# One order of work for another: the two written sequences of a transformer block

## The chip, the cores and the metric

The kernel runs on one core of a Trainium2 chip. The metric is the device time of one execution in microseconds (us). Five engines matter: TensorE (PE in the profile; its weight loads are PEld), VectorE (DVE), ScalarE (ACT), GpSimd (POOL) and SyncE (SP), which here only issues DMAs. SP and POOL each have a queue of DMAs that go out in order. Each engine runs its own instructions in order and waits on semaphores for the others.

## The reference

One block on 512 tokens of width 1024, in fp32: a norm, one wide projection, a gated linear attention (GLA, 4 heads) and a latent attention (MLA, 8 heads) side by side, their gated sum through `w_out`, then a squared-ReLU MLP of width 4096 and a last norm.

```python
n = rmsnorm(h, g_mix)
proj = n @ w_in
(gq, gk, gv, gr, z_gf, z_gb, cq, ckv, kr, z_ma, z_mb) = jnp.split(proj, SPLIT_IDX, axis=-1)
y_gla = gla_branch(gq, gk, gv, gr, z_gf, z_gb, ...)
y_mla = mla_branch(cq, ckv, kr, positions, g_q, w_uq, g_kv, w_ukv)
merged = jax.nn.sigmoid(z_ma) * y_gla + jax.nn.sigmoid(z_mb) * y_mla
h = h + merged @ w_out
m = rmsnorm(h, g_mlp)
h = h + jnp.square(jax.nn.relu(m @ w_ff1)) @ w_ff2
return rmsnorm(h, g_final)
```

In `mla_branch` each head has 64 features without and 32 with rotary position; `cq` and `ckv` are normed and then multiplied up to queries, keys and values; each head takes a softmax over all 512 tokens.

## The kernel before

Every fp32 matrix is held as a rounded upper part and a rest (names in h and l), and each product is three matmuls (`mm3`: high by high, high by low, low by high). The large products (projections, `w_out`, the MLP) use a scheme with seven half-size products instead of eight, so their operands are sums of blocks (names such as bo10 to bo71 for the right operands of `w_out`, gao, gbo, gco, gdo, yo, zo for the left).

What sets the order: nothing is scheduled. While `nc.hold()` is on, each call on an engine is recorded under a letter and the name of its first tile (`P` TensorE, `A` ScalarE, `D` VectorE, `G` GpSimd, `S` SyncE's DMAs; `D:h0` is VectorE's next recorded call that writes h0). `nc.emit(SEQUENCE)` then issues the recorded calls as the string names them, `*3` meaning three in a row, and `in_program_order` keeps each engine to that order. So only the place of an entry among the entries of the same letter matters, and each queue stands still while its first entry waits. SEQUENCE covers the stretch from the last GLA head to the first products of the MLP; LAST_ROWS covers the last rows of the MLP and the final norm.

What is in the stretch, with the names that matter:

- `up_units(pr)` makes queries, keys and values for the heads 2pr and 2pr+1. Its weights come through a stage buffer (`stage`, three buffers in all, also used by `streamed` for the weights bo.. of `w_out`), are split (wq..h/l, wk..h/l), and give uq, uk and uv in PSUM. The rotary part of q is copied by DMA from ro (`rotary_rows`), the other head's half of q and of the keys (kbuf) by DMA too. For the last pair, pr = 3, the weights of q are wq3f; the keys lie in four tiles kbuf0 to kbuf3, of which heads 4 to 7 reuse those of heads 0 to 3.
- `att_scores` computes s (head, block of 128 queries), VectorE's row maximum top and ScalarE's exponential e with its sum tot; `att_normalise` takes the reciprocal and scales e, one block on ScalarE and one on VectorE; `att_flip` transposes e into tp and splits it into pT (ScalarE high, VectorE low); `att_values` gives av, `merge` gates it (tb, VectorE) and adds the GLA part on GpSimd into mx and my; `merged_sums` forms yo and zo from these.
- `wo_product` adds the products with bo.. into the accumulators wox, wow and woz (a bank each for row block 0 and 1); `add_rows` adds a full bank into h on VectorE (`D:h0`), after which the bank may be used anew.
- Then the MLP's norm: ScalarE squares the rows of h with their sum (ms), VectorE combines (hp), GpSimd raises hp to the power −1/2, VectorE and ScalarE scale the rows (ms again), and TensorE flips them into the banks mb. The flipped rows are split into mh and ml for f0x, the MLP's first product.
- `load_onto` adds a block of weights in DRAM onto a tile in SBUF with an accumulating DMA from GpSimd's queue (`G:w2_20`); plain loads go through SyncE's queue.

Of the kernel before, what the change touches and what calls it, by code (L numbers as in the profile page):

```python
# [97 lines left out]
def tile_block(ctx: ExitStack, tc: tile.TileContext, t, out: bass.AP):  # L98
# [1784 lines left out]
    for x in range(2):  # L1883
        f0.lo(2, x)
        m_lo(2, x)
    SEQUENCE = """
# [5 lines left out]
        A:tb4 P:ro1*9 S:wk1f D:ckvhl1 A:zb7h D:sc1 D:gla3s D:rob0 D:rob1 D:sc0 D:zb7l P:zb6*24 A:wk1h S:wq2f
        A:kbuf0 G:wk1l A:ckvhl0 D:kbuf0 A:wk1h D:roa0 S:kbuf2 G:wk1l P:uq0*9 D:roa0 S:w2_11 A:q010 G:wk0l A:ro0
        G:wk0l P:gla3o0*12 D:ro0 G:wk0l D:ckvhl0 S:q001 P:gla3o1*12 S:w2_10 D:roa1 P:gla3o1*6 S:q000 D:roa1
        P:gla3o0*6 S:kbuf1 A:ro1 S:q010 A:gla3sq D:ro1 A:wk1h P:uk0*6 S:q000 G:wk1l A:kbuf0 S:q001 G:wk0l A:wk1h
        S:q010 A:tb5 S:q111 A:q000 A:gla3sq S:wq2f D:q001 A:kbuf1 S:q011 D:q011 A:gla3sq*2 S:wq1f D:zb6 A:yg4
        G:gla3ss*2 S:wq1f D:kbuf0 G:gla3ss S:wq1f G:wk1l D:grc P:zb7*24 S:wq2f D:zb7 S:q011 P:s00*3 D:grb S:q111
        D:kbuf1 S:w2_20 D:grc P:uv01*12 D:top00 S:q210 A:v01 P:s03*3 D:grb S:bo11f A:wq1h A:e00 P:s01*3 S:q110
        G:wq1l D:top01 A:wq2h S:bo11f D:v01 G:wq2l S:bo10f P:uk1*6 D:top03 A:kbuf2 P:y16*4 A:yg6 S:wk2f P:y17*4
        A:e03 P:s11*3 S:w2_00 D:top11 A:e01 S:kbuf3 P:s02*3 S:q211 A:e11 D:tot00 P:s10*3 S:w2_30 D:top10 A:e00  # L1900
        S:q110 D:top02 A:e10 S:w2_01 D:kbuf2 A:e02 P:uq1*9 A:q100 D:tot02 P:s13*3 A:yg7 S:q110 P:s12*3 A:bo11h
        D:q101 S:kbuf3 D:e01 S:q111 D:top13 S:bo10f P:uv10*12 D:tot10 D:bo11l P:tp000*4 S:q210 A:pT000 P:tp001*3
        A:e02 D:top12 S:wk3f A:e13 D:pT010 S:q100 P:uv00*12 P:tp001 P:uq2 A:v00 S:q100 A:e12 D:v00 S:q101 A:e10
        D:tot12 D:e03 S:kbuf2 A:wk2h P:uq2*8 D:e13 A:wk2h G:wk2l S:q101 A:pT001 G:wk2l S:w2_00 A:wk2h A:e12 S:w2_01
        G:wk2l P:uv11*12 P:tp010*4 S:q211 A:pT000 P:s31*3 A:v10 D:top31 P:tp011*4 A:tb7 D:pT010 A:e31 D:e11 P:uk2*6
        D:pT011 A:pT001 P:tp101*4 A:q200 D:pT011 P:tp100*4 A:wk3h S:q210 A:pT101 D:v10 P:s21*3 A:pT100 D:q201
        P:s20*3 A:wk2h P:av0 D:top20 A:kbuf0 S:q211 G:wk2l D:top21 A:wk3h S:w2_20 A:v11 S:w2_10 D:pT111 A:e20
        S:bo21f D:kbuf0 P:av0*11 A:e21 S:q200 D:pT110 P:tp110*4 S:kbuf1 D:tot20 A:pT100 D:e21 P:s23*3 A:bo10h
        S:q201 D:top23 P:s22*3 S:q201 D:pT110 A:e23 P:tp111*4 D:top22 A:pT101 D:tb0 A:e22 P:uv21*12 D:pT111 G:mx0
        A:e20 P:s30*3 D:tot22 A:e22 G:my0 D:top30 P:s32*3 D:bo10l G:w2_20 A:e30 P:tp200*4 G:wk3l A:pT200 S:wq3f  # L1910
        D:pT210 S:kbuf0 D:e23 S:q200 D:top32 P:av1*12 S:wq3f D:tb1 A:e32 P:tp201*4 S:wq3f P:s33*3 G:my0 A:wk3h
        A:pT201 S:q311 D:top33 P:tp210*4 G:mx0 A:v21 S:q311 D:v11 P:s53*3 A:pT200 S:bo21f D:pT211 A:e33 S:q310
        D:v21 A:wk3h P:uv20*12 S:h2 D:pT210 A:wq3h P:tp211*4 S:q300 D:top53 G:wq3l P:s41*3 S:q310 P:av2 D:tot30
        D:e31 A:e53 S:q301 P:s40*3 G:wk3l A:e30 D:tot32 D:top41 S:w2_30 A:pT201 G:wk3l D:top40 S:q301 P:av2*5 A:tb6
        G:w2_00 P:uq3 S:w2_31 P:tp301*4 G:wk3l A:pT301 S:bo20f A:e41 S:w2_21 D:pT311 A:e40 S:w2_21 P:uq3*8 S:q300
        P:tp300*4 D:tot40 D:pT211 A:pT300 S:w2_11 P:s51*3 A:q300 D:top51 S:w2_31 P:s43*3 D:e33 S:bo20f A:e51
        P:s42*3 D:top43 S:w221f A:v20 D:pT310 A:e32 P:av2*5 D:top42 D:v20 P:s52*3 A:e42 D:q301 P:tp311*4 A:pT301
        D:e41 A:e43 D:top52 P:uv30*12 A:gao0 D:pT311 A:e52 P:s50*3 G:gao0 P:av2 A:e40 D:tb2 P:tp310*4 A:pT300
        D:tot52 D:tot42 G:yo0 D:e43 A:q310 P:uk3*6 G:mx1 D:pT310 A:kbuf3 P:tp400*4 D:q311 A:kbuf2 G:w2_21 P:tp401*4
        A:pT400 D:top50 G:yo0 A:pT401 D:kbuf2 A:e42 D:kbuf3 G:my1 A:e50 D:pT411 G:zo0 P:av3*12 A:v30 D:tb3 P:s70*3  # L1920
        D:pT410 G:my1 P:tp410*4 A:pT400 D:tot50 D:top70 P:s60*3 G:w2_20 A:e50 D:pT410 P:tp411*4 G:zo1 A:pT401 D:v30
        A:e70 D:top60 G:mx1 P:uv31*12 A:e52 D:pT411 G:yo1 A:e60 P:s61*3 P:av4 D:top61 G:yo1 A:gdo0 P:s63*3 A:bo50h
        D:e51 D:top63 P:s62*3 A:e61 D:top62 P:wox0*3 A:e63 D:tot60 P:tp501*4 D:e53 A:e62 D:bo50l P:wox1*3 A:pT501
        P:tp511*4 D:tot62 A:gao1 D:e61 S:w2_00 P:s71*3 D:pT511 A:ghyo0 G:gao1 S:h0 A:pT501 D:top71 P:av4*4 S:h1
        A:bo21h D:gdo0 P:s72*3 S:h3 G:zo1 D:pT511 A:e71 D:top72 G:glyo0 A:e60 P:av4*7 D:tb4 P:tp500*4 A:pT500
        P:tp510*4 D:tot70 D:e63 G:my2 A:pT500 D:pT510 P:s73*3 P:wox0 A:e72 D:pT510 G:mx2 P:wox0*2 A:e62 D:bo21l
        P:tp601*4 G:w2_11 A:v31 P:tp600*4 P:av5 A:pT601 G:w2_21 P:av5*2 D:top73 A:pT600 G:zo0 P:tp610*4 A:e70
        D:pT610 A:pT600 D:pT611 A:ghyo1 G:zo2 D:e71 A:e73 P:av5*9 D:tb5 P:tp611*4 A:pT601 D:tot72 D:pT610 P:wox1*3
        G:my2 A:gdo0 P:tp700*4 D:pT611 A:ghzo1 G:glyo1 P:tp701*4 P:av6 D:v31 A:pT701 D:e73 A:pT700 G:mx2 A:bo20h
        D:pT710 G:yo2 D:pT711 A:e72 P:av6*11 G:w2_01 D:bo20l A:f010h P:av7*5 G:yo2 A:gao2 D:tb6 P:av7*7 D:gao2  # L1930
        G:w2_10 P:wow0*3 G:mx3 P:tp710*4 A:pT700 P:wow0*3 A:ghyo2 G:zo2 D:pT710 P:tp711*4 A:pT701 G:my3 P:wox1*3
        A:gao3 P:wox0*3 D:gao3 D:gdo0 P:woz1*3 D:tb7 D:pT711 G:mx3 P:wox0*3 D:f010l P:wox1*3 A:bo60h G:w2_00 A:gao3
        D:bo60l P:av7*12 P:wow1*3 D:gao3 P:wow0*3 D:zo3 D:tb7 P:woz0*3 D:glyo2 G:my3 P:wow1*3 A:bo61h P:wow0*3
        G:w2_20 D:yo3*2 P:woz1*3 G:glzo1 D:h0 P:woz0*3 D:h1 A:bo51h D:zo3 P:wow1*3 P:wox0*3 A:ghbo3 D:bo51l A:ghco3
        P:wox0*3 D:glbo3 P:wow1*3 S:w2_01 A:bo31h D:h0 P:woz0*3 D:h1 P:woz0*3 A:ms0 D:bo31l A:gdo2 P:wox1*3 G:hp0
        A:ms1 P:wox1*3 D:bo61l A:ghzo0 S:w2_31 P:woz1*3 A:bo71h G:glzo0 D:h2 P:woz1*3 A:bo30h D:h3 P:wox0*3 G:hp1
        G:w2_21 P:wox1*3 A:ghzo2 D:bo30l A:f011h P:wox0*3 D:glco3 P:wox1*3 S:w2_30 A:bo70h D:glzo2 S:w220f D:h0
        D:bo70l P:woz0*12 D:bo71l D:h1 S:w2_11 A:bo40h D:h0 S:w2_10 P:woz1*12 A:ms0 D:h1 A:gdo2 D:hp0 D:bo40l A:ms1
        G:hp0 P:wox1*6 A:f050h D:ms0 A:ms0 D:hp1 D:f011l G:hp1 P:wox0*12 G:w2_01 A:ms1 P:mb02 P:mb01 D:h2 P:mb03
        A:bo41h D:ms1 D:gdo2 P:wox1*6 D:gdo2 P:mb03 P:mb02 P:mb00 P:mb01 D:bo41l P:mb00 P:mb02 P:mb01 P:mb00*2  # L1940
        P:mb02 P:mb03 A:mr20 P:mb03 P:mb01 D:h3 A:mr10 A:mr21 D:f050l A:mr11 A:ms2 A:mr10 G:w2_00 A:mr11 A:mr21
# [128 lines left out]
```

## Time and profile before

| | before |
|---|---|
| runs (us) | 737.14, 738.35, 738.58; median 738.35 |
| the profiled execution (us) | 737.48 |
| its span, first to last instruction (us) | 735.8 |
| granted clock of TensorE | 0.998 |
| mean DMA rate | 149 GB/s |

The span is what the rows of the profile lie in, from 0 to 735.8; the 1.7 us around it have no rows. The stretch that SEQUENCE orders lies between about 253 and 422 us. Rows give the start, the duration, the engine, the source line (held calls all have L76, the line in `emit`), the operation, the names out<-in without buffer numbers, and in brackets the idle time just before with what ended it. TensorE's rows overlap, since matmuls are pipelined: the step from one start to the next is the cost, not the duration.

### The profile page before, as it was taken

Reading aid. Unit: us, or ns where it says so; the run is one execution under the profiler, and the core shown is the slowest. Engines: PE = TensorE matmul, PEld = TensorE weight load, DVE = VectorE, ACT = ScalarE, POOL = GpSimd, SP = SyncE. Lnnn points to the kernel's source line nnn. Section 1 sums busy time; section 2 is a strip of 40 time slices with the busy share of each in tenths; the row PEclk is TensorE's granted clock in tenths of the full one; section 3 lists DMA queues with packets and bytes.
Section 4 is the critical chain, followed back from the end, with each engine's and each line's share of the span. In section 5 each row is a group of like instructions: output and inputs, shape, how many; then the busy total and the mean of one; then the engine's idle time right before and its main releaser. Section 6 shows DMA issues by size and latency. Waiting matters only on the chain.

```text
span 735.8 us, 11339 instructions
## 1 busy us (share of the span) xinstructions
PE 725.2 (99%) x4142; PEld 637.7 (87%) x4142; DVE 622.4 (85%) x861; ACT 495.1 (67%) x809; POOL 223.6 (30%) x284
## 2 busy tenths in 40 slices
...
...
GB/s 311 276 125 207 211 178 88 86 59 29 58 58 58 61 73 115 215 164 220 178 125 209 135 216 192 190 217 55 244 183 204 3 230 198 201 58 143 173 98 131
DMA packets 81191, 109.93 MB, mean 149 GB/s; under 512 B 16208, under 2 KB 34640, under 8 KB 81136
## 3 DMA queue, kind: packets, MB, share of 16 engines
...
## 4 chain that ended last, share of the span: by engine, by line
PE 91%; DVE 3%; ACT 1%; issue 1%; DMA 1%; POOL 1%; SPq 0%; POOLq 0%; DVEq 0%; ACTq 0%
PE f3x L90 3%; PE f2x L90 3%; PE f1x L90 3%; PE f0x L90 3%; PE wox L76 3%; PE first L90 3%; PE g2x L90 3%; PE g1x L90 3%; PE g0x L90 3%; PE gvx L90 3%; PE zax L90 3%; PE grx L90 3%; PE s L76 2%; PE av L76 2%; PE gk L90 2%; PE cq L90 2%
## 5 line engine op out<-in xcount | busy, mean ns | idle before, releaser
...
L76 PE MATMUL s<-kbuf,q 96*128 96x512 f32 x96 | 27.0, 404 | 1.1 <-DMA wq3f<-in_w_uq 0.9
L76 DVE TENSOR_REDUCE top<-s 128x1 f32<-128x512 f32 x32 | 21.6, 683 | 5.4 <-PE s L76 5.2
L76 PE MATMUL av<-pT,v 128*128 128x512 f32 (+1 forms) x108 | 24.9, 372 | 0.0
L76 DVE TENSOR_TENSOR pT<-tp,pT 128x512 fp32r<-128x512 f32 x32 | 21.4, 681 | 3.8 <-ACT pT L76 3.4
L76 ACT ACTIVATE e<-s,top 128x512 f32<-128x512 f32 x32 | 21.9, 691 | 3.2 <-DVE top L76 3.1
L76 ACT ACTIVATE pT<-tp 128x512 fp32r<-128x512 f32 x32 | 18.6, 601 | 5.3 <-PE tp L76 5.2
L76 PEld LDWEIGHTS av<-pT,v 128*128 128x128 f32 x108 | 18.6, 189 | 3.3
L76 PEld LDWEIGHTS s<-kbuf,q 96*128 96x128 f32 x96 | 16.8, 189 | 4.5 <-issue 1.1
L76 PE MATMUL tp<-ident,e 128*128 128x128 f32 x128 | 18.4, 272 | 0.0
L76 PEld LDWEIGHTS tp<-ident,e 128*128 128x128 f32 x128 | 15.4, 140 | 3.2 <-DVE pT L76 0.3
...
L90 POOL TENSOR_TENSOR qF<-qk,qF 128x512 fp32r<-128x512 f32 x3 | 5.3, 1761 | 32.8 <-ACT qF L90 32.8
...
L90 DVE TENSOR_TENSOR w<-w,w 128x1024 f32<-128x1024 f32 x12 | 14.4, 1220 | 0.1
L76 ACT ACTIVATE ms<-h 128x512 f32<-128x512 f32 (+1 forms) x17 | 10.3, 605 | 5.0 <-DVE h L76 4.9
L76 POOL TENSOR_TENSOR hp<-hp,mhalf 128x1 f32<-128x1 f32 x8 | 9.0, 1129 | 13.0 <-DVE hp L76 12.8
...
L76 ACT ACTIVATE e<-e,tot 128x512 f32<-128x512 f32 x16 | 11.5, 725 | 0.0
L90 ACT ACTIVATE f2h<-f2a 128x512 fp32r<-128x512 f32 x10 | 6.1, 621 | 6.2 <-DVE f2a L90 6.2
(1945 smaller groups left out, 3089.8 us busy)
## 6 DMA issues: line engine op xcount, KB each, us to landing
...
w221f<-in_w_ff SPq DMA_DIRECT2D x8, 512.0 KB, 5.2
```

The source lines that it names most:

```text
L76: what(*args, **options)
L90: return what(*args, **options)
```

## The change

Both strings are replaced; every entry of the old SEQUENCE occurs in the new one as often. No call, tile, buffer or size changes. The first of SEQUENCE's some 60 lines, before and after, and the two lines of LAST_ROWS that differ:

```diff
     SEQUENCE = """
-        S:zb6f S:wr0f*3 A:sin D:cqc1 S:wk0f D:cqc2 P:bd*4 A:bds A:zb6h P:sc0*5 A:wr0h P:sc1*5 D:sc1 A:cqhl1 G:wr0l
...
+        S:w2_11 S:zb6f S:w2_01 S:wr0f*2 A:sin A:zb6h D:cqc2 S:wk0f D:zb6l S:wr0f P:bd*4 D:cqc0 S:wr1f P:sc0*5
...
     LAST_ROWS = """
...
-        D:g370l P:g3x0*6 D:f3l70 P:g3x1*3 D:h0 P:g3x1*3 D:f3l71 A:ms0 G:ms0 D:h1 P:g3x1*3 A:ms0 D:h1 P:g3x0*3
-        A:g340h D:f3l41 G:hp0 P:g3x0*3 A:ms1 D:hp0 D:g340l P:g3x0*3 G:hp0 A:ms1 P:g3x1*3 A:g341h D:f3l40 G:hp1
+        D:g370l P:g3x0*6 D:f3l70 P:g3x1*3 D:h0 P:g3x1*3 D:f3l71 A:ms0 G:ms0 D:h1 P:g3x1*3 A:g340h D:h1 P:g3x0*3
+        A:ms0 D:f3l41 G:hp0 P:g3x0*3 A:ms1 D:hp0 D:g340l P:g3x0*3 G:hp0 A:ms1 P:g3x1*3 A:g341h D:f3l40 G:hp1
```

In LAST_ROWS that swap of ms0 and g340h on ScalarE is all. In SEQUENCE most entries have moved by a few places. Three places follow with the engine's rows before and now. In them q_635 and q_636 are the queries of head 4 (high and low), q_637 and q_638 those of head 5, q_711 and q_712 belong to the last pair; kbuf_530 is kbuf0 and kbuf_531 kbuf1.

First, SyncE's queue ahead of the first scores of head 4. `kbuf_530<-kbuf_531` is the copy of the keys' rotary rows that these scores read, `q_635<-ro` and `q_636<-ro` the rotary rows of the queries. Before:

```order
L76 DMA bo21f_2813<-in_w_out 128x512
L76 DMA q_635_2660<-ro_556_2581 16x512
L76 DMA kbuf_531_2556<-kbuf_530_2555 64x1024
L76 DMA q_636_2661<-ro_556_2581 16x512
L76 DMA q_636_2661<-ro_559_2584 16x512
L76 DMA wq3f_2730<-in_w_uq 128x2x64
L76 DMA kbuf_530_2555<-kbuf_531_2556 32x1024
L76 DMA q_635_2660<-ro_559_2584 16x512
L76 DMA wq3f_2730<-in_w_uq 128x2x64 x2
```

Now, from the weights of the last pair on:

```order
L76 DMA wq3f_2730<-in_w_uq 128x2x64 x2
L76 DMA q_712_2737<-ro_556_2581 16x512
L76 DMA h_872_2897<-in_x 128x1024
L76 DMA bo10f_2696<-in_w_out 128x512 x2
L76 DMA wq3f_2730<-in_w_uq 128x2x64
L76 DMA kbuf_531_2556<-kbuf_530_2555 64x1024
```

and the copies, further on:

```order
L76 DMA q_637_2662<-q_635_2660 64x512
L76 DMA w_10_801_2826<-in_w_out 128x512
L76 DMA q_636_2661<-ro_556_2581 16x512
L76 DMA q_635_2660<-ro_556_2581 16x512
L76 DMA q_635_2660<-ro_559_2584 16x512
L76 DMA kbuf_530_2555<-kbuf_531_2556 32x1024
L76 DMA q_636_2661<-ro_559_2584 16x512
```

The three loads of wq3f stood around the copies and now stand ahead of them, two of them also ahead of bo10f, which uses a stage buffer too; the rows of q stand with the copy of kbuf.

Second, VectorE at the first sums from wox into h (h_869 is h0, h_870 is h1), which empty the banks wox_844 and wox_845; yo_884 is yo3. Before:

```order
L76 TENSOR_TENSOR glyo_866_2891<-yo_838_2863,ghyo_865_2890 128x512
L76 TENSOR_TENSOR yo_884_2909<-my_860_2885 128x256
L76 TENSOR_TENSOR yo_884_2909<-yo_884_2909,mx_859_2884 128x256
L76 TENSOR_TENSOR h_869_2894<-h_869_2894,wox_844_2869 128x512
L76 TENSOR_TENSOR h_870_2895<-h_870_2895,wox_845_2870 128x512
L76 TENSOR_TENSOR zo_885_2910<-mx_859_2884,yo_884_2909 128x256
L76 TENSOR_TENSOR bo51l_2914<-w_01_721_2746,bo51h_2913 128x1024
```

Now:

```order
L76 TENSOR_TENSOR bo60l_2916<-w_20_735_2760,bo60h_2915 128x1024
L76 TENSOR_TENSOR h_870_2895<-h_870_2895,wox_845_2870 128x512
L76 TENSOR_TENSOR gao_877_2902<-mx_859_2884,gao_877_2902 128x256
L76 TENSOR_TENSOR glyo_866_2891<-yo_838_2863,ghyo_865_2890 128x512
L76 SCALAR_TENSOR_TENSOR tb_577_2602<-tb_577_2602,av_863_2888 128x256
L76 TENSOR_TENSOR h_869_2894<-h_869_2894,wox_844_2869 128x512
L76 TENSOR_TENSOR bo31l_2928<-w_31_804_2829,bo31h_2927 128x1024
L76 TENSOR_TENSOR yo_884_2909<-my_860_2885 128x256
L76 TENSOR_TENSOR yo_884_2909<-yo_884_2909,mx_859_2884 128x256
```

Both sums from wox now stand ahead of yo's two steps; on GpSimd a step glzo of zo1 followed the last my3 and an issue, and now a glzo of zo0 does, whose other operand, ghzo0, ScalarE writes after the first squares ms; that of zo1 stands behind it and an hp.

Third, VectorE around the powers of the first two row blocks: hp_896 and hp_898 go to GpSimd, which returns them to ms_897 and ms_899. Before:

```order
L76 TENSOR_TENSOR h_869_2894<-h_869_2894,woz_875_2900 128x512
L76 TENSOR_TENSOR h_870_2895<-h_870_2895,woz_876_2901 128x512
L76 SCALAR_TENSOR_TENSOR hp_896_2921<-hp_896_2921 128x1
L76 TENSOR_TENSOR bo40l_2942<-w_20_735_2760,bo40h_2941 128x1024
L76 TENSOR_SCALAR ms_897_2922<-h_869_2894,hp_896_2921 128x512
L76 SCALAR_TENSOR_TENSOR hp_898_2923<-hp_898_2923 128x1
L76 TENSOR_TENSOR f011l_2940<-w_01_721_2746,f011h_2939 128x1024
L76 TENSOR_TENSOR h_871_2896<-h_871_2896,wox_844_2869 128x512
L76 TENSOR_SCALAR ms_899_2924<-h_870_2895,hp_898_2923 128x512
```

Now:

```order
L76 TENSOR_TENSOR h_870_2895<-h_870_2895,woz_876_2901 128x512
L76 TENSOR_TENSOR gdo_905_2930<-my_860_2885,gdo_905_2930 128x256
L76 SCALAR_TENSOR_TENSOR hp_896_2921<-hp_896_2921 128x1
L76 TENSOR_TENSOR gdo_904_2929<-my_659_2684,gdo_904_2929 128x256
L76 TENSOR_SCALAR ms_897_2922<-h_869_2894,hp_896_2921 128x512
L76 SCALAR_TENSOR_TENSOR hp_898_2923<-hp_898_2923 128x1
L76 TENSOR_TENSOR h_871_2896<-h_871_2896,wox_844_2869 128x512
L76 TENSOR_SCALAR ms_899_2924<-h_870_2895,hp_898_2923 128x512
L76 TENSOR_TENSOR bo41l_2944<-w_21_736_2761,bo41h_2943 128x1024
L76 TENSOR_TENSOR gdo_904_2929<-my_739_2764,gdo_904_2929 128x256
L76 TENSOR_TENSOR bo40l_2942<-w_20_735_2760,bo40h_2941 128x1024
L76 TENSOR_TENSOR f011l_2940<-w_01_721_2746,f011h_2939 128x1024
```

The two long splits bo40l and f011l stood each behind an hp and now stand behind both ms; a step gdo and the sum from wox stand there instead. On TensorE the flips of row block 1, which read ms_899, now follow those of block 0 without the six wox matmuls that stood between them.

More of the change, by code (lines that the diff above doesn't have):

```diff
@@ L1892, in tile_block @@
[L1892 to L1941, printed above, removed]
@@ new lines, in tile_block @@
+        P:gla3o0*6 A:gla3sq S:wq1f A:wk1h P:gla3o1*6 A:zb7h S:q000 G:wk1l S:q001 A:gla3sq P:uk0*6 D:zb7l A:gla3sq
+        S:q211 A:q000 S:q110 A:kbuf0 S:wq2f P:uv01*12 A:kbuf1 D:kbuf0 S:q110 A:gla3sq A:v01 G:gla3ss S:kbuf2
+        G:gla3ss A:wq1h S:q011 A:wk1h G:gla3ss A:q010 G:wq1l S:q010 D:grc D:grb S:q010 D:kbuf1 S:wq2f D:q011
+        S:w2_10 D:q001 S:wk2f D:grb D:v01 S:q011 P:zb7*24 D:zb7 S:q211 P:s00*3 D:grc S:q210 P:s01*3 S:w2_20 D:top01
+        S:w2_30 D:top00 S:wq2f A:e00 P:uq1*9 A:tb4 P:y17*4 A:q100 P:y16*4 A:e01 P:s03*3 S:q110 D:top03 A:wk2h
@@ new lines, in tile_block @@
+        A:wk2h A:pT000 P:s31*3 G:wk2l A:tb7 P:tp011*4 D:top31 S:wq3f A:wk3h P:tp100*4 P:av0 D:pT010 A:q200 S:wq3f
+        A:e31 D:q201 D:tot12 P:uk2*6 D:e13 A:kbuf0 P:tp101*4 S:q301 A:pT001 P:s21*3 S:h3 A:wk2h D:pT011 A:e12
+        G:wk2l D:top21 A:pT101 S:bo10f A:pT100 D:pT111 S:bo10f A:e21 P:av0*11 D:pT110 S:wq3f A:wk3h P:tp110*4
+        D:kbuf0 A:pT100 P:s20*3 A:v11 D:pT110 S:kbuf1 P:s23*3 S:w2_00 D:top23 P:s22*3 S:q211 D:tb0 A:e23 P:tp111*4
+        S:q210 D:top20 G:my0 A:pT101 S:q210 D:top22 A:e20 G:mx0 P:uv20*12 S:w2_10 D:pT111 A:bo10h P:s33*3 D:tot20
@@ new lines, in tile_block @@
+        G:wk3l S:bo21f A:e52 D:e53 P:s41*3 P:uq3 S:w2_30 G:wk3l P:tp301*4 D:top41 S:q310 A:pT301 D:v20 S:bo21f
+        A:e41 P:av2*5 D:top42 S:w2_01 A:v21 S:q311 A:pT300 D:v21 S:w2_21 D:pT310 P:uq3*8 S:w2_11 A:q300 D:tot40
+        P:s51*3 P:av2 A:e42 S:q300 D:top51 P:tp310*4 S:q301 D:tb2 A:pT300 S:w2_31 A:e51 D:tot42 D:pT310 P:uk3*6
+        S:q311 A:e40 D:e43 S:w2_21 P:s50*3 D:e41 A:q310 G:my1 D:pT311 S:q310 P:tp311*4 A:pT301 P:tp401*4 D:top50
+        G:mx1 S:bo20f A:e42 D:pT311 S:w2_31 A:wk3h D:q311 A:kbuf2 G:wk3l A:e50 D:kbuf2 G:yo0 A:pT401 D:tot50
@@ new lines, in tile_block @@
+        P:av3*12 D:q301 G:zo1 A:kbuf3 P:tp400*4 D:pT411 G:w2_20 A:pT400 P:tp410*4 A:pT400 P:s61*3 G:w2_11 D:top61
+        P:s60*3 G:w2_01 D:top60 A:e61 D:kbuf3 A:e60 P:uv31*12 D:pT410 A:bo50h P:tp411*4 P:av4 D:tb3 A:pT401 P:s62*3
+        D:tot60 D:pT410 G:mx1 A:e60 D:top62 G:yo0 D:e51 A:e62 G:my1 P:uv30*12 D:pT411 A:v31 P:s63*3 G:yo1 D:top63
+        A:e50 P:s71*3 A:ghyo0 D:e61 G:w2_21 D:top71 A:e63 P:av4*4 G:w2_20 D:bo50l A:e71 P:tp510*4 P:tp500*4 A:pT500
+        D:tot62 P:s70*3 S:w2_00 A:v30 D:top70 P:tp600*4 S:h2 A:gao1 D:e63 A:pT500 S:h0 D:pT510 G:gao1 A:pT600 S:h1
@@ new lines, in tile_block @@
+        A:gao2 G:zo1 D:pT711 A:f010h P:av6*11 G:zo2 D:tb6 P:wow1*3 D:gao2 G:mx3 P:tp710*4 A:pT700 P:wow0*3 A:ghyo2
+        D:pT710 G:w2_21 A:gao3 P:av7*7 D:f010l G:w2_10 P:wow1*3 D:gao3 P:wow0*3 G:w2_00 D:bo21l P:tp711*4 A:pT701
+        P:wox1*3 A:bo60h D:tb7 D:pT711 P:wox1*3 G:mx3 A:gdo0 D:bo60l P:wox0*3 G:my3 A:ghzo2 A:gao3 A:ghzo1 D:h1
+        P:av7*12 D:gao3 D:glyo2 P:wox0*3 A:bo31h D:tb7 P:wow1*3 D:h0 G:my3 P:wox1*3 D:bo31l A:gdo2 P:wow0*3
+        P:woz1*3 D:yo3*2 P:wow1*3 D:h1 P:wow0*3 D:zo3 A:bo51h D:h0 P:woz0*6 A:ghbo3 D:bo51l A:bo61h P:wox0*3 D:zo3
@@ new lines, in tile_block @@
+        P:wox1*3 S:w2_01 A:ms1 D:glbo3 S:w221f P:wox0*3 A:ms0 D:bo61l A:ghzo0 P:woz0*3 A:bo30h G:glzo0 P:woz0*3
+        D:h2 P:woz1*3 D:bo30l G:w2_21 P:wox1*3 G:hp0 P:wox1*3 G:glzo1 D:h1 P:wox0*3 D:glzo2 P:woz1*3 G:w2_20
+        A:bo71h P:wox0*3 D:h0 A:ghco3 A:bo70h D:glco3 D:h3 D:bo70l P:woz0*12 D:bo71l A:bo41h D:h0 S:w2_11 D:gdo2
+        P:woz1*12 A:ms0 S:w2_10 D:h1 S:w2_30 A:gdo0 D:gdo2 A:ms1 S:w220f D:hp0 D:gdo0 G:hp0 A:bo40h S:w2_31 G:hp1
+        D:ms0 D:hp1 A:ms0 P:wox0*12 G:hp1 D:h2 A:ms1 D:ms1 A:f011h P:wox1*6 D:bo41l P:mb02 P:mb01 P:mb02 P:mb00
@@ L1945, in tile_block @@
+        P:mb01 P:mb00 P:mb02 P:mb00*2 D:gdo0 P:mb03 G:w2_10 A:mr10 D:bo40l A:ms2 A:f050h P:wox1*6 G:hp2 D:f011l
+        P:mb03 P:mb02 P:mb01 P:mb03*2 P:mb01 A:mr21 A:mr10 D:h3 A:f020h D:f050l A:mr11 A:mh1 A:mr11 P:wox0*12
+        A:mr21 D:h2 A:ms3 D:ml1 A:mr20 G:hp3 A:mh1 G:w2_01 A:mr20 D:ml1 A:mh2 G:w2_00 P:wox1*12 A:ms2 D:ml2 A:mh2
+        D:h3 A:f021h D:hp2 D:f020l G:hp2 A:ms3 D:hp3 D:ms2 G:hp3 D:ms3 D:ml2 A:f051h D:f021l D:f051l G:w2_01
+        G:w2_11
     """
```

29 lines of the change are left out of this document (22 added, 7 removed).

## The prediction

> **What bounds the kernel now.** I read the page first, from the top: the busy shares, then the chain that ended last. After that came the list of what TensorE waited for, and then the rows around each of those waits. The page's two lines:
>
> ```profile
> PE 725.2 (99%) x4142; PEld 637.7 (87%) x4142; DVE 622.4 (85%) x861; ACT 495.1 (67%) x809; POOL 223.6 (30%) x284
> PE 91%; DVE 3%; ACT 1%; issue 1%; DMA 1%; POOL 1%; SPq 0%; POOLq 0%; DVEq 0%; ACTq 0%
> ```
>
> TensorE is busy for 725.2 of 735.8 us, and 91% of the chain is its own work. The change issues the same matmuls, so all that an order can win is the time in which TensorE waits. That list is short; its columns are total, times and longest, in us:
>
> ```profile
> PE warm L90 <- POOL ident masks.py:199: 1.5, 1, 1.5
> PE wox L76 <- DVE h L76: 1.1, 1, 1.1
> PE s L76 <- DMA wq3f<-in_w_uq: 0.9, 1, 0.9
> PE s L76 <- DVE grc L76: 0.2, 1, 0.2
> ```
>
> The first is at the start of the program, which the change leaves alone. The other three lie in the stretch that SEQUENCE orders. Their sum, 1.1 + 0.9 + 0.2 = 2.2 us, is the most that can be won from waits the list shows. The matmuls that end them (the bracket is the idle time just before):
>
> ```profile
> 291.98 0.98 PE L76 MATMUL s<-kbuf,q 96*128 96x512 f32 x3 [0.17 <-DVE grc L76]
> 329.33 0.93 PE L76 MATMUL s<-kbuf,q 96*128 96x512 f32 x3 [0.94 <-DMA wq3f<-in_w_uq]
> 385.99 0.50 PE L76 MATMUL wox<-bo60h,ghyo 128*128 128x512 f32 x1 [1.06 <-DVE h L76]
> ```
>
> So the question of this change is whether these three go, and whether the new order puts others in their place.
>
> **The wait at 329.33 (s41, the first scores of head 4).** It is put down to a load of wq3f, but the load is not what s41 reads: it reads kbuf and q. SyncE's queue and its waits tell it:
>
> ```profile
> SPq L76 <- DVE bo10l L76: 4.0, 1, 4.0
> 322.37 0.38 SPq L76 DMA_DIRECT2D wq3f<-in_w_uq  x1
> 322.86 0.51 SPq L76 DMA_DIRECT2D kbuf<-kbuf  x1
> 323.42 0.89 SPq L76 DMA_DIRECT2D q<-ro  x1
> 321.00 1.27 DVE L76 TENSOR_TENSOR bo10l<-bo10f,bo10h 128x1024 fp32r<-128x1024 f32 x1
> kbuf<-kbuf SPq DMA_DIRECT2D x1, 128.0 KB, 5.6
> 321.13 1.28 POOL L76 DMA_DIRECT2D w<-in_w_out  x1
> ```
>
> The load needs a stage buffer, which VectorE's bo10l frees when it ends at 321.00 + 1.27 = 322.27. Until then the queue stands for 4.0 us, and behind the load stand the kbuf copy and the rotary rows of q that head 4 needs. The copy takes 5.6 from its issue: 322.86 + 5.6 = 328.5. The q rows, issued 0.56 later, land last, and s41 starts at 329.33. In the changed order the first two wq3f loads stand before both loads of bo10f and so wait for an earlier buffer; the third stands behind them but well ahead of the copies. The copies then have rows of q, two w_out tiles and no blocked load ahead of them. If the queue stands 4.0 us less, the copies land up to 4.0 us sooner, against a wait of 0.9. GpSimd's accumulating load, which issued 1.7 us before the copy (321.13) and whose 512 KB moved at the same time, is gone from there; the next of its kind stands behind the second pair of merge sums instead of the first. The term: −0.9. Bounds: 0 (the copies are as late as now for another reason) and −0.94.
>
> **The wait at 385.99 (wox, refilled after its first sums into h).** Here wox needs the bank that VectorE's sum into h empties:
>
> ```profile
> 382.62 0.43 DVE L76 TENSOR_TENSOR yo<-my 128x256 f32<-128x256 f32 x1 [0.63 <-POOL my L76]
> 383.08 2.26 DVE L76 TENSOR_TENSOR yo<-yo,mx 128x256 f32<-128x256 f32 x1
> 385.27 1.27 DVE L76 TENSOR_TENSOR h<-h,wox 128x512 f32<-128x512 f32 x2
> 386.46 0.41 DVE L76 TENSOR_TENSOR zo<-mx,yo 128x256 f32<-128x256 f32 x1
> 383.31 1.74 POOL L76 TENSOR_TENSOR glzo<-zo,ghzo 128x512 fp32r<-128x512 f32 x1
> ```
>
> The second step of yo takes 2.26 where zo, of the same form, takes 0.41: stretched by 1.85. It ends at 385.34, and GpSimd's glzo beside it at 383.31 + 1.74 = 385.05. In front of it VectorE also idled 0.63 for GpSimd's my. The sums into h queue behind both. In the changed order each sum that frees a wox bank stands ahead of yo's two steps, and the glzo that GpSimd has next needs ghzo0, which ScalarE writes only after its first squares ms. Either would do alone: 0.63 + 1.85 = 2.5 exceeds the 1.06. The term: −1.1. Bounds: 0 and −1.1.
>
> The rule of the Trainium skill's page "SBUF — State Buffer", section "Who interferes with whom", says that a VectorE instruction with two SBUF inputs contends with a GpSimd instruction that reads SBUF, since they share a port pair that is locked as a whole. The trace agrees (2.26 against 0.41); by it glzo can still stretch such a step, but none that frees a bank, since those have one input in PSUM.
>
> **The wait at 291.98 (s01).** It follows these two steps of VectorE on the output of the last GLA head, whose bank s01 takes:
>
> ```profile
> 291.44 0.48 DVE L76 SCALAR_TENSOR_TENSOR grc<-gla3o,gla3ss,grc 128x256 f32<-128x256 f32 x1
> 292.44 0.47 DVE L76 SCALAR_TENSOR_TENSOR grb<-gla3o,gla3ss,grb 128x256 f32<-128x256 f32 x1
> ```
>
> In the new order both steps of grb and one of grc stand ahead of zb7's drain, and s01 behind zb7's 24 matmuls. At the step of 0.23 that two neighbours show (386.33, 386.56) these are 5.5 us of cover; the chain to the second grb, counted with the durations of before, leaves some 0.5 of it.
>
> ```profile
> 386.33 0.39 PE L76 MATMUL wox<-bo60l,ghyo 128*128 128x512 f32 x1
> 386.56 0.40 PE L76 MATMUL wox<-bo60h,glyo 128*128 128x512 f32 x1
> ```
>
> The term: −0.2, bounds 0 and −0.2.
>
> **The powers.** GpSimd raises the mean squares to −1/2 (hp). The rows, GpSimd's first:
>
> ```profile
> 401.46 1.48 POOL L76 TENSOR_TENSOR hp<-hp,mhalf 128x1 f32<-128x1 f32 x1 [6.66 <-DVE hp L76]
> 403.60 1.47 POOL L76 TENSOR_TENSOR hp<-hp,mhalf 128x1 f32<-128x1 f32 x1 [0.67 <-DVE hp L76]
> 414.17 0.56 POOL L76 TENSOR_TENSOR hp<-hp,mhalf 128x1 f32<-128x1 f32 x1 [2.20 <-DVE hp L76]
> 401.28 1.22 DVE L76 TENSOR_TENSOR bo40l<-w,bo40h 128x1024 fp32r<-128x1024 f32 x1
> 403.44 1.22 DVE L76 TENSOR_TENSOR f011l<-w,f011h 128x1024 fp32r<-128x1024 f32 x1
> 405.30 0.48 DVE L76 TENSOR_SCALAR ms<-h,hp 128x512 f32<-128x512 f32 x1
> ```
>
> Beside the sums bo40l and f011l a power takes 1.48 and 1.47 (it ends 0.4 after the sum); with VectorE idle beside it, 0.56. The change puts both sums behind both powers, so I price them at 0.56. This is no gain by itself: TensorE has no wait there now. It is the cover for another edit. The flips of row block 1 (mb) come six wox matmuls and two flips sooner, 6 × 0.23 + 2 × 0.11 = 1.6 us. Before, ms of block 1 ends at 405.30 + 0.48 = 405.78, and the flip that reads it, the sixth of the 13 that start at 406.21, is at 406.8: a margin of 1.0.
>
> ```profile
> 406.21 1.58 PE L76 MATMUL mb<-ident,ms 128*128 128x128 f32 x13
> ```
>
> Now that flip is due at 405.15. With powers of 0.56 the chain ends at 405.78 − 2 × 0.92 + 0.4 (one gdo that now stands in it) = 404.3: 0.8 to spare, term 0. With 1.48 both times it would end at 406.2 and TensorE would wait 1.0. What stands beside the powers now is gdo, 0.4 long, and h, 0.7 long; ended 0.4 after these, the powers take some 0.7 and 0.9, which together costs 0.5 and still leaves 0.3. I take 0 and keep +1.0 as the upper bound.
>
> **The rest.** The other moves (load order of w_out, which head's scores stand first, the swap of ms0 and g340h in LAST_ROWS) carry no row of a wait now. Following the new order with the durations of before, I find no wait but several margins under 0.3 us, of which some will open by 0.1: +0.2, bounds 0 and the rival below. Sum: −1.1 − 0.9 − 0.2 + 0.0 + 0.2 = −2.0. On the profiled execution, 737.48 (its span 735.8 and 1.7 around it), that gives 735.5. This execution lies 0.87 under the median of the three runs, 738.35, and the mean of all four is 737.9; from that mean the sum gives **735.9**.
>
> **The rivals.** (A) The powers stay long, and the flips of block 1 wait 1.0 us: 735.9 + 1.0 = 736.9. For it: 1.48 in two of the rows above, and less distance. Against it: the sums that went with the 1.48 are gone from beside them.
>
> (B) A gathered copy is late at another place. The copies of heads 2 and 3 stand behind loads into stage buffers in the same queue; a copy takes 5.6, and a blocked issue costs as much as it did here, 0.9, on top of the forecast: 736.8. Against it: the one long standing of the queue in this window, 4.0, is the one that is undone.
>
> (C) Slower, by one mechanism: GpSimd steps beside VectorE's chain around 337 to 345, where the last scores of heads 4 and 5 are normalised and flipped. Now GpSimd is idle there:
>
> ```profile
> 341.61 1.29 POOL L76 TENSOR_TENSOR gao<-mx,gao 128x512 fp32r<-128x512 f32 x1 [7.32 <-ACT gao L76]
> 342.86 0.74 POOL L76 TENSOR_TENSOR yo<-my 128x256 f32<-128x256 f32 x1
> 340.03 0.47 DVE L76 TENSOR_SCALAR e<-e,tot 128x512 f32<-128x512 f32 x1
> 342.92 0.96 DVE L76 TENSOR_SCALAR e<-e,tot 128x512 f32<-128x512 f32 x1
> ```
>
> After 7.32 idle its first steps come, and the normalisation beside yo takes 0.96 instead of 0.47. The new order brings my1, mx1, wk3l, yo0 and zo1 into that chain, whose margins I put at about 0 to 0.2. One stretch of 0.5 costs 0.3 to 0.5. Three of the size seen at 383.08, 1.85 each, cost 5.5 less 0.4 of margin and moved steps: 735.9 + 5.1 = 741.0; two cost 739.2. It decides from stretches of 2.4 on, the 2.0 won and 0.4 of margin. Against it: the sums that flip (pT) read a PSUM bank, and only the normalisations and the late yo steps were seen stretched.
>
> By the same section of the Trainium skill a step with a PSUM input and one SBUF input does not contend at all, which leaves the two normalisations of that chain, 0.5 each by the row: 736.9 in place of 741.0. The row agrees as far as it goes.
>
> (D) The change does not do what it says: the three waits go and return at the next place where TensorE is tight, so the time stays at 737.9. For it: a program that is 99% TensorE has only small margins. Against it: no wait on a weight or a bank follows in the list, up to the end.
>
> **How the numbers follow.** Chances: the forecast 0.58, A 0.12, B 0.10, C 0.13, D 0.07. What a measurement of this kernel tells from no change is about 0.2%, 1.5 us, so faster means below 736.9 and slower above 739.8. Faster: nearly all of the forecast (0.55) and a third of A and B (0.07), in all 0.62. Slower: the two- and three-stretch cases of C, 0.11. Same: the remaining 0.27. The range: below, all three waits gone, no new one, and a run as low as the lowest one is under the mean, 737.14 − 737.9 = −0.8, gives 735.7 − 0.8 = 734.9; above, two stretches of C, 739.2. That leaves out the three-stretch case and a run still lower.
>
> **What would show it.** Right: the list of TensorE's waits holds only the first of its four rows and rows under 0.3; the two copies before s41 land 2 us or more ahead of it; yo's second step may stay long but no wox waits for h; the two powers take under 1.0. Wrong: a wait of TensorE on h, ms or pT of 0.5 or more (A, C), on a kbuf or q copy (B), or a span that falls by less than the waits that went, with TensorE's busy time grown (D).

## The result, and the profile after

| | before | changed |
|---|---|---|
| median (us) | 738.22 of 6 runs (737.14 to 738.58) | 734.64 of 6 runs (734.48 to 734.92) |
| ratio | | 0.9955, 95% interval 0.9942 to 0.9968 |
| profiled execution, its span (us) | 737.48, 735.8 | 734.56, 732.8 |
| chain: share of TensorE | 91% | 96% |

The change is faster by 3.6 us in the medians and by 2.9 in the profiled executions; both lie in the interval (2.4 to 4.3 us). A later set of runs gave 734.63 against 738.12 (run after_again), the same ratio. The forecast was 735.9 with a range from 734.9: right in direction, short in size, and the range missed the time by 0.3.

The page after, busy times and chain:

```profile
PE 724.4 (99%) x4142; PEld 637.6 (87%) x4142; DVE 624.0 (85%) x861; ACT 494.2 (67%) x809; POOL 224.3 (31%) x284
PE 96%; DVE 2%; issue 1%; POOL 0%; ACT 0%; POOLq 0%; DVEq 0%
```

And the whole list of TensorE's waits after (total, times, longest in us):

```profile
PE warm L90 <- POOL ident masks.py:199: 1.5, 1, 1.5
```

The three other rows are gone and none has come in their place. That the gain lies in the stretch of SEQUENCE alone shows in its first and last rows. Before:

```profile
253.90 1.05 PE L76 MATMUL bd<-qkb 128*128 128x128 f32 x8
420.58 0.36 PE L90 MATMUL f0w<-mh,f020h 128*128 128x256 f32 x1
```

After:

```profile
254.03 1.05 PE L76 MATMUL bd<-qkb 128*128 128x128 f32 x8
417.64 0.36 PE L90 MATMUL f0w<-mh,f020h 128*128 128x256 f32 x1
```

From bd to f0w it is 166.68 before and 163.61 after: 3.07 less. From f0w to the last matmul both take 308.03. The time from bd to f0w is the measure used below for every run, since it repeats far better than the time of the whole does: five profiled executions of before gave 166.68, 166.67, 166.44, 166.51 and 166.74 (mean 166.61, against which the runs below stand), three of the changed kernel 163.61, 163.60 and 163.61.

**s43, now the first scores of head 4.** SyncE's queue, GpSimd's load, the scores, and the landing times of the copy and of the load in this stretch:

```profile
324.88 0.52 SPq L76 DMA_DIRECT2D kbuf<-kbuf  x1
325.44 0.59 SPq L76 DMA_DIRECT2D q<-ro  x1
327.22 1.28 POOL L76 DMA_DIRECT2D w<-in_w_out  x1
328.96 1.53 PE L76 MATMUL s<-kbuf,q 96*128 96x512 f32 x6
kbuf<-kbuf SPq DMA_DIRECT2D x1, 128.0 KB, 2.3
w<-in_w_out POOLq DMA_DIRECT2D x1, 512.0 KB, 5.7
```

The copies do not issue sooner, as the prediction had it. They issue 2.0 us later than before (324.88 against 322.86), and land all the same 1.3 sooner, at 327.2, since they take 2.3 instead of 5.6. What is different is that the load of 512 KB now stands behind them, not ahead.

**The first sums into h.** VectorE, GpSimd and the two wox after:

```profile
379.87 0.39 PE L76 MATMUL wox<-bo60h,ghyo 128*128 128x512 f32 x1
377.99 0.68 DVE L76 TENSOR_TENSOR h<-h,wox 128x512 f32<-128x512 f32 x1
379.85 0.68 DVE L76 TENSOR_TENSOR h<-h,wox 128x512 f32<-128x512 f32 x1
382.21 0.42 DVE L76 TENSOR_TENSOR yo<-yo,mx 128x256 f32<-128x256 f32 x1
380.01 0.75 POOL L76 TENSOR_TENSOR my<-tb,yg 128x256 f32<-128x256 f32 x1 [1.34 <-DVE tb L76]
387.94 1.30 POOL L76 TENSOR_TENSOR glzo<-zo,ghzo 128x512 fp32r<-128x512 f32 x1 [7.18 <-ACT ghzo L76]
384.63 0.39 PE L76 MATMUL wox<-bo60h,ghyo 128*128 128x512 f32 x1
```

The first sum ends at 378.67, 1.2 ahead of the wox that needs its bank at 379.87 (the first row above), the second at 380.53, 4.1 ahead of its own, the last row. yo's second step takes 0.42, with glzo not before 387.94.

**The powers**, GpSimd's and VectorE's rows after:

```profile
398.94 0.67 POOL L76 TENSOR_TENSOR hp<-hp,mhalf 128x1 f32<-128x1 f32 x1 [5.79 <-DVE hp L76]
400.46 0.56 POOL L76 TENSOR_TENSOR hp<-hp,mhalf 128x1 f32<-128x1 f32 x1 [0.28 <-DVE hp L76]
400.47 0.69 DVE L76 TENSOR_TENSOR h<-h,wox 128x512 f32<-128x512 f32 x1
401.08 0.48 DVE L76 TENSOR_SCALAR ms<-h,hp 128x512 f32<-128x512 f32 x1
```

They take 0.67 beside the short gdo and 0.56 beside h, which reads a PSUM bank; before, 1.48 and 1.47. The Trainium skill's page "SBUF — State Buffer", section "Who interferes with whom", has a VectorE step with at most one SBUF input, outside its two-port modes, leave GpSimd alone; the 0.56 beside h agrees.

### The profile page after: what moved, and what is told of

The parts are those of the page before. It is cut to its first block, busy times and chain, and to the rows that moved or that the text cites. A ratio compares the mean times of both kernels' runs of the same rounds, so it can differ in the third digit from the quotient of the medians.

```text
span 732.8 us, 11339 instructions
## 1 busy us (share of the span) xinstructions
PE 724.4 (99%) x4142; PEld 637.6 (87%) x4142; DVE 624.0 (85%) x861; ACT 494.2 (67%) x809; POOL 224.3 (31%) x284
## 4 chain that ended last, share of the span: by engine, by line
PE 96%; DVE 2%; issue 1%; POOL 0%; ACT 0%; POOLq 0%; DVEq 0%
PE f3x L90 3%; PE f2x L90 3%; PE f1x L90 3%; PE f0x L90 3%; PE first L90 3%; PE s L76 3%; PE av L76 3%; PE wox L76 3%; PE g2x L90 3%; PE g1x L90 3%; PE g0x L90 3%; PE gvx L90 3%; PE zax L90 3%; PE grx L90 3%; PE gk L90 2%; PE cq L90 2%
## 5 line engine op out<-in xcount | busy, mean ns | idle before, releaser
L76 POOL TENSOR_TENSOR my<-tb,yg 128x256 f32<-128x256 f32 x8 | 7.2, 899 | 13.7 <-DVE tb L76 7.5
```

The costliest lines, as they stand in the source:

```text
L76: what(*args, **options)
```

## Where 3.0 us come from when the list of waits adds up to 2.2

The list counts idle time, from the modelled end of a matmul to the start of the next. But TensorE runs matmuls overlapped, each start 0.23 behind the last, while a row lasts 0.39. A wait costs what lies between the starts. Rows of before at s01 and at wox (the row of s01 at 291.98 and those of wox at 385.99 and 386.33 stand in the prediction):

```profile
290.95 0.86 PE L76 MATMUL s<-kbuf,q 96*128 96x512 f32 x3
292.79 0.62 PE L76 MATMUL uk<-ckvhl,wk1h 128*128 128x512 f32 x2
384.54 0.39 PE L76 MATMUL wow<-bo21h,gao 128*128 128x512 f32 x1
```

At wox, 385.99 − 384.54 = 1.45, less the usual 0.23, is 1.22; and the next start, 0.34 on instead of 0.23, adds 0.11: 1.33 in all, where the list has 1.06. At s01, 1.03 from 290.95 to 291.98 for three matmuls instead of 0.69, and 0.81 from there to 292.79, make 0.46, where the list has 0.17 (0.44 in the table, by 0.233, the usual step of this form). Counted so from all of TensorE's starts in the stretch, the waits come to this, each with the slow step behind it:

| place | before | after |
|---|---|---|
| uk0 (VectorE's roa1) | 0.17 | – |
| s01 (VectorE's grc or grb) | 0.44 | 0.11 |
| s41, then s43 (copies) | 1.18 | – |
| wox (VectorE's h) | 1.33 | – |
| sum | 3.12 | 0.11 |

The difference, 3.01, is the gain of 3.07 within 0.06. Besides these, some 30 single steps in either kernel (34 before, 30 after) are 0.06 to 0.09 longer than usual and one after is 0.10 longer, with no idle time before them; they are left out of the table, and with all the rest they make the 0.06. uk0 is in no row of the list: its idle time lies under the overlap.

## The experiments

Every run is an order of the same instructions: no work is left out in any. The time of a run stands against that of before in the same set: 737.89 for three, copies, sums and again; 738.12 for after_again, five, late_load and early_load; 738.13 for the others.

**three, copies, sums: the moves one by one.** The edits (three has all of them):

```diff
-  S:wq3f D:pT210 S:kbuf0 D:e23 S:q200 D:top32 P:av1*12 S:wq3f
+  D:pT210 S:kbuf0 D:e23 S:q200 D:top32 P:av1*12 S:wq3f*2
...
-  D:yo3*2 P:woz1*3 G:glzo1 D:h0 P:woz0*3 D:h1 A:bo51h D:zo3
+  D:h0 D:h1 D:yo3*2 P:woz1*3 G:glzo1 P:woz0*3 A:bo51h D:zo3
...
-  D:kbuf1 S:w2_20 D:grc
+  D:grc D:kbuf1 S:w2_20
```

> The order before with three local moves only: the copies kbuf0 and q200 ahead of the wq3f loads, the two sums into h ahead of yo's two steps, grc ahead of kbuf1. Theory (three places are all): counted from start to start, with the slow second step behind each wait, these cost 0.44 + 1.24 + 1.33 = 3.0 us in the profile of before, so the time falls by 3.0 to 3.6, to 734.6 to 735.2, level with the changed kernel. Rival (the list of waits is the full price, the rest of the new order earns what is left): it falls by 2.2, to 736.0, and stays 1.4 above the changed kernel.

> The order before with one move: the copies kbuf0 and q200 ahead of the wq3f loads in SyncE's queue. Theory (s41 waits for the copies, which stood behind a blocked load): the wait at s41 goes, 1.2 us by the steps, to about 737.0. Rival 1 (by the list, 0.9): 737.3. Rival 2 (the load or the DMA engines' traffic makes it late, not the queue): no change, 738.2, and the copies land as late as before.

> The order before with one move: the two sums from wox into h ahead of yo's two steps on VectorE; GpSimd's glzo stays beside yo. Theory (the order alone decides): yo's second step still takes about 2.3, no matmul waits for h, and the time falls by 1.3 by the steps, to 736.9. Rival (the stretched step is only moved: zo3, bo51l and what reads them are late by as much): a new wait on one of them of 0.5 to 1.1, and a gain under 0.8.

Measured: three 735.74 (ratio 0.9969, 0.9957 to 0.998), copies 736.91 (0.9986, 0.9977 to 0.9995), sums 737.20 (0.9988, 0.998 to 0.9997). From bd to f0w three takes 164.74, copies 165.55, sums 166.00: 1.9, 1.1 and 0.6 under before. copies does what it should: kbuf0 issues at 320.47, 2.4 sooner and ahead of the load, lands in 2.3, and s41 does not wait. sums does half of it, and three comes out 1.1 above the changed kernel. Half of that is in three's waits and in its rows of VectorE and GpSimd:

```profile
PE woz L76 <- DVE bo51l L76: 0.3, 1, 0.3
382.05 2.25 DVE L76 TENSOR_TENSOR yo<-my 128x256 f32<-128x256 f32 x1
382.27 1.74 POOL L76 TENSOR_TENSOR glzo<-zo,ghzo 128x512 fp32r<-128x512 f32 x1
385.13 1.22 DVE L76 TENSOR_TENSOR bo51l<-w,bo51h 128x1024 fp32r<-128x1024 f32 x1
```

glzo still stretches a step of yo, now the first one, to 2.25. The sums into h are out of its way, but bo51l behind it is late, and woz waits 0.53 by the steps. That is the rival written down for sums: the stretched step is only handed on. The other half has no row in the list. uk0's 0.17 is still there, and at the first scores of head 2, at 311.46 (s21; the expectation of four calls the place s30), the steps cost 0.38 more than in before: the copy into kbuf lands at 311.33 instead of 309.14 and the rows of q at 312.04 instead of 309.40, each 0.13 ahead of a matmul that starts late. SyncE's queue stands 2.9 there for copies q<-q, 0.6 in before. The runs copies and four (below), which each share one or two of the moves, do not have the wait; what makes it is open.

**glzo_off and five: glzo taken away from yo.** glzo_off moves it behind the next hp; five has the edits of three, this one, and roa1 ahead of roa0's second step.

```diff
-  D:yo3*2 P:woz1*3 G:glzo1 D:h0
+  D:yo3*2 P:woz1*3 D:h0
...
-  P:wox1*3 G:hp0 A:ms1
+  P:wox1*3 G:hp0 G:glzo1 A:ms1
```

> The order before with one move on GpSimd: glzo of zo1 behind the next hp; VectorE's sums into h stay behind yo. Theory (yo is long because glzo runs beside it): yo's second step takes 0.43, not 2.26, wox does not wait, 1.33 gained; glzo then stretches bo30l as in the run five, which costs 0.5: net 0.8, to 737.2. Rival (yo is long by itself, or the order behind it is the cause): yo stays above 2, wox still waits 1.1, 738.0.

> The order before with five local moves: the three of the run called three, and GpSimd's glzo of zo1 behind the next hp (so that yo is not stretched and bo51l not late), and roa1 ahead of roa0's second step (so that uk0 does not wait). By the steps of the run three these two are worth 0.53 and 0.17. Theory (single waits are the whole of the change): 735.7 - 0.7 = 735.0, at most 0.5 above the changed kernel, TensorE's list of waits empty but for warm. Rival (the rest of the new order matters by itself): it stays at 735.7, 1.1 above the changed kernel.

Measured: glzo_off 736.66 (0.9983, 0.9974 to 0.9993), five 735.44 (0.9966, 0.9952 to 0.998). VectorE and a wait of glzo_off:

```profile
382.76 0.42 DVE L76 TENSOR_TENSOR yo<-yo,mx 128x256 f32<-128x256 f32 x1
391.93 1.93 DVE L76 TENSOR_TENSOR bo30l<-w,bo30h 128x1024 fp32r<-128x1024 f32 x1 [0.37 <-ACT bo30h L76]
PE woz L76 <- DVE bo30l L76: 0.2, 1, 0.2
```

yo is 0.42 and wox does not wait: 1.33 won, shown to be glzo's doing. But the two glzo then run one behind the other from 389.36 on, bo30l beside them takes 1.93 instead of 1.23, and woz waits 0.50 by the steps. five has that wait too, and another; its list names

```profile
PE s L76 <- DMA q<-ro: 0.3, 1, 0.3
PE woz L76 <- DVE bo30l L76: 0.2, 1, 0.2
```

The first is the wait at s21 again, 0.49 by the steps. three has 0.38 there without roa1's move, so that move accounts for some 0.1 of it at most; it was not tried apart. roa1 does what it should, and uk0's 0.17 is gone. five keeps 2.05 of the 3.0, 0.2 more than three: glzo's move only put a wait of 0.50 in the place of 0.53, and the wait at s21 stayed, so its expectation was missed.

**four: the moves with glzo where nothing is behind it.** glzo goes behind the mx3 ahead of it; s41 is freed by moving the load, as in late_load below; grc and the sums as in three.

```diff
-  G:mx3 P:wox0*3 D:f010l
+  G:mx3 G:glzo1 P:wox0*3 D:f010l
```

> The order before with four local moves whose followers the runs so far have shown: w2_20's load as in late_load, grc ahead of kbuf1 and the sums into h ahead of yo as in three, and glzo of zo1 already behind the mx3 before it, where nothing long follows on VectorE's way to a bank. Theory (single waits are the whole of the change): s41 gives 1.18, wox 1.33, s01 0.44 less the 0.3 that three lost again at s30: 2.65 off the profile, within 0.5 of the changed kernel, 735.0 to 735.3. Rival (the rest of the new order is worth 1 us by itself): not under 735.7.

Measured: 735.25 (0.9958, 0.9945 to 0.997), and 163.72 from bd to f0w, 0.11 above the changed kernel. In its profile only warm is left in the list of waits. Four moves in an order of some 1,500 calls thus give all but 0.1 us of what the change wins in this stretch: it is the single waits that count, and not the new order as a whole. The median lies 0.6 above that of the changed kernel, from runs that scatter from 734.55 to 736.12; its profiled execution has 0.6 of it ahead of the stretch, in a longer start of the kind described at the end of this section. The stretch was not saved but laid where it is free:

```profile
376.62 2.27 POOL L76 TENSOR_TENSOR glzo<-zo,ghzo 128x512 fp32r<-128x512 f32 x1
378.31 1.67 DVE L76 TENSOR_TENSOR bo60l<-w,bo60h 128x1024 fp32r<-128x1024 f32 x1 [0.57 <-ACT bo60h L76]
```

**late_load and early_load: the queue or the load.** late_load is before with one entry of GpSimd moved, early_load the changed kernel with the entry moved the other way:

```diff
-  D:bo10l G:w2_20 A:e30
+  D:bo10l A:e30
...
-  P:tp210*4 G:mx0 A:v21
+  P:tp210*4 G:mx0 G:w2_20 A:v21
```

```diff
-  A:e20 G:mx0 P:uv20*12
+  A:e20 G:mx0 G:w2_00 P:uv20*12
...
-  D:top53 G:w2_00 D:pT210
+  D:top53 D:pT210
```

> The order before with one move on GpSimd: the accumulating load of w2_20 behind the second pair of merge sums; SyncE's queue keeps its block of 4.0 us. Theory 1 (the copies are late because that load's 512 KB move ahead of theirs): kbuf0 and q200 issue at 322.9 and 323.4 as now, land within 2.5 instead of 5.6, before 326, s41 does not wait, and the time falls by 1.2, to 736.7. Theory 2 (the queue's block alone is the cause, as the prediction put it): the copies still take 5 or more, s41 waits 0.9, no change: 737.9.

> The changed order with one move on GpSimd: its accumulating load of w2_00 ahead of the second pair of merge sums, so that it issues around 322.6, 2.3 ahead of the copies kbuf0 (324.9) and q201 (325.4). Theory 1 (that load makes copies behind it slow): they take 4 to 6 instead of 2.2, land around 330, and s43, which starts at 329.0 now, waits 0.8 to 1.8: 735.4 to 736.4. Theory 2 (only the queue matters): no wait, 734.6.

Measured: late_load 737.10 (0.9986, 0.9977 to 0.9994), 165.49 from bd to f0w, 1.1 under before. early_load 735.87 (0.9967, 0.9956 to 0.9979), 164.62, 1.0 above the changed kernel. late_load's queue and copy:

```profile
322.81 0.38 SPq L76 DMA_DIRECT2D wq3f<-in_w_uq  x1
323.31 0.51 SPq L76 DMA_DIRECT2D kbuf<-kbuf  x1
kbuf<-kbuf SPq DMA_DIRECT2D x1, 128.0 KB, 2.3
```

early_load's copy, and its s43:

```profile
kbuf<-kbuf SPq DMA_DIRECT2D x1, 128.0 KB, 5.2
330.28 1.62 PE L76 MATMUL s<-kbuf,q 96*128 96x512 f32 x6 [0.72 <-DMA kbuf<-kbuf]
```

In late_load the queue stands as long as in before, and the copies are even later by 0.45, but take 2.3 and no matmul waits. In early_load a load 2.2 us ahead of the copy makes it 5.2 and the wait is back. Theory 1 holds on both sides, and copies fits it: there the copy issues 1.05 ahead of the load and takes 2.3. The Trainium skill's page "DMA: Bandwidth & Descriptors", section "Issuing engines are not separate DMA queues", says that DMAs of all issuing engines run on the same 16 engines and interleave; these rows agree that a load of one queue delays a copy of another, and give the price here, about 3 us. The delayed copy lands only behind the load (328.46 against 327.32 in before, 330.15 against 329.33 in early_load), so how far the two interleave these rows do not show.

**splits_beside_powers and glzo_beside: what covers what in the changed order.** Both are the changed kernel with one thing put back.

```diff
-  D:hp0 D:gdo0 G:hp0
+  D:hp0 D:bo41l D:gdo0 G:hp0
...
-  D:hp1 A:ms0 P:wox0*12
+  D:hp1 D:bo40l A:ms0 P:wox0*12
```

```diff
-  G:my3 P:wox1*3 D:bo31l
+  G:my3 G:glzo1 P:wox1*3 D:bo31l
...
-  P:wox1*3 G:glzo1 D:h1
+  P:wox1*3 D:h1
```

> The changed order with VectorE's long sums bo41l and bo40l put back beside the two powers, one behind each hp. Theory (a long sum of two SBUF operands stretches the power, and the changed order has used up the distance that covered it): powers of about 1.5 instead of 0.67 and 0.56, ms of block 1 ends 1.9 later, against 0.73 of margin at its flip: TensorE waits about 1.2 there and the time rises to 735.8. Rival (the cover is larger than counted, or the powers stay short): no wait, 734.6.

> The changed order with GpSimd's glzo of zo1 put directly behind the last my3, so beside bo31l and yo. Theory (with the sums into h ahead, the stretch is only handed on): a step of VectorE there takes about 2 instead of 0.4 or 1.4, no matmul waits for the wox sums, but bo51l, whose margin is 1.06, is late and a woz matmul waits 0.3 to 0.9: 734.9 to 735.5. Rival 1 (the order alone makes it harmless): no wait, 734.6. Rival 2 (it costs what it cost before): 1.3, to 735.9.

Measured: splits_beside_powers 735.97 (0.9968, 0.9956 to 0.998) and 164.72 from bd to f0w, 1.1 above the changed kernel; glzo_beside 734.81 (0.9951, 0.9939 to 0.9964) and 163.62, level with it. The first one's powers and its wait:

```profile
398.87 1.47 POOL L76 TENSOR_TENSOR hp<-hp,mhalf 128x1 f32<-128x1 f32 x1 [5.79 <-DVE hp L76]
401.20 1.48 POOL L76 TENSOR_TENSOR hp<-hp,mhalf 128x1 f32<-128x1 f32 x1 [0.28 <-DVE hp L76]
PE mb L76 <- DVE ms L76: 0.9, 1, 0.9
```

So the powers are worth nothing in the change by themselves, and 1.1 us as the cover of the flips that it moved ahead. glzo_beside, VectorE and GpSimd:

```profile
382.07 1.51 DVE L76 TENSOR_TENSOR yo<-my 128x256 f32<-128x256 f32 x1
381.02 2.28 POOL L76 TENSOR_TENSOR glzo<-zo,ghzo 128x512 fp32r<-128x512 f32 x1
```

The collision is there again, 1.1 on yo, and nobody waits: against the theory, which had bo51l's margin of 1.06 used up. bo51l in fact begins at 385.49 instead of 384.61, 0.9 later, and the margin just holds. In the changed order glzo's place is therefore free at this spot; in the order before it cost 1.3.

**Before and after once more.** after_again and after_2 are the changed kernel; again, before_2, before_3 and before_4 are before. No edit.

> The changed kernel, unchanged, as the measure for the runs beside it. Its profile lost 3.0 us against the profile of before, its median 3.6. Theory (the executions of before vary by its waits, those of this one cannot): 734.6 again, with a spread under 0.6, while before spreads over 1.3 or more. Rival (that was the chip of that day): a spread like that of before.

> The changed kernel, unchanged, one more profiled execution. Theory: from the 40th of the first matmuls on it takes 711.2, as twice before, whatever the first 13 us take. Rival: a surplus of 0.3 or more in the stretch that was laid out anew.

> The kernel before once more, unchanged, for a second profiled execution. The six runs of before lie between 737.1 and 738.6 and those of the changed kernel between 734.5 and 734.9. Theory (the three waits vary): if this execution is longer than the first profile's 737.48, the surplus stands in TensorE's waits before s41 or wox, and the rows behind f0w take as long as in the first profile. Rival (the spread is elsewhere): those waits stay at 0.9 and 1.1 within 0.1 and the surplus lies in another part of the program.

> The kernel before, unchanged, one more profiled execution (one of three). Theory: from the 40th of the first matmuls on it takes 714.3, give or take the wait at s41, and what is above that lies either in the first 13 us or in that wait. Rival: a wait of 0.3 or more at a place where no profile so far shows one.

> As for before_2: the same kernel once more, with the same two answers (714.3 and the surplus in the first 13 us or at s41, or a new wait of 0.3 or more).

> As for before_2: the same kernel once more, with the same two answers (714.3 and the surplus in the first 13 us or at s41, or a new wait of 0.3 or more).

Measured: the executions of before took 737.51, 737.52, 738.03 and 738.44, those of the changed kernel 734.96 (after_2) and 734.63 in the median of after_again (734.58 to 735.12, before beside it 737.01 to 739.25). In all profiles the part behind f0w takes 308.03 to 308.07. From TensorE's first matmul to bd it takes 252.36 to 253.24 in before and 252.50 to 253.00 in the changed kernel, and the scatter arises in the first 13 us. There the first products stand 0.43 to 0.57 apart instead of 0.23, four or five such steps in the longest executions and one or none in the shortest; the list names no wait there, and why it is so is not shown. Behind these products before takes 714.1 to 714.3 and the changed kernel 711.2, as expected. The s41 wait scatters too: 0.95 to 1.22 by the steps in these executions, 0.71 in glzo_off, which does not touch it. No other place varies by more than 0.05. So both sources of the theory hold. Not settled is the last half microsecond: five profiled executions of before average 737.80 and three of the changed kernel 734.85, 2.95 apart, while the medians of the timed runs are 3.5 to 3.6 apart. What before does in its executions of 739 no profile here has caught, and whether the rest of the new order has a part in it is open.

## Where the prediction was right, and which step of it failed

- **That TensorE's waits bound the gain, that three places carry it and that all three are gone**: right but for uk0, a fourth place with 0.17 (the list after; four; five).
- **The term 1.1 + 0.9 + 0.2 = 2.2 was mis-sized**, and this is the step that failed. "Their sum … is the most that can be won from waits the list shows" took idle time for cost. From the starts the three places cost 1.33, 1.18 and 0.44 (0.11 of the last is left), and uk0's 0.17 was missed: 3.0. The rows were at hand, and so was the rule: the flips were priced from start to start, the waits were not.
- **"+0.2" for margins that open**: 0.0 measured beyond what is left at s01; the list after is empty. With both put right, the sum would have been −3.0 and the forecast 734.9; the lower end, set 0.8 under it for the scatter of single runs, would have held 734.64.
- **s41: the wait goes**, right; **the reason, copies up to 4.0 sooner as the queue stands less**, wrong. They issue 2.0 later; the load that the prediction mentioned as a second point decides (late_load, early_load). Copies that no longer stand behind the blocked load in the queue also come in time (copies), as they then issue ahead of the 512 KB, but that is not what the change does. The sign "2 us or more ahead" was missed too: the two copies land at 327.17 and 327.54, 1.8 and 1.4 ahead of the scores.
- **wox: "Either would do alone"**: right of the wait at wox, wrong of the time. The sums alone hand 0.53 on to bo51l, glzo alone hands 0.50 on to bo30l (sums, glzo_off). The changed order does both, and has the margins to carry a collision besides (glzo_beside).
- **s01 with 0.5 of cover**: too much; in the rows after, the second grb ends at 291.03, 0.06 ahead of s01, and a slow step of 0.11 is left there.
- **Powers, term 0, with 1.0 as the price if they stay long**: right: 0.67 and 0.56, and 1.1 when put back.
- **Rival A** did not come, since the sums stood elsewhere. **B** did not come. **C** did not come: GpSimd's first step there is at 340.45, none of VectorE's steps from 337 to 345 is stretched, and no flip waits. **D** fell: the gain by the rows of TensorE is kept to the last matmul.
